# Loading and working the last two rows of each partition as half rows in a row-sum of reciprocals

## The chip, the cores and the metric

The kernel runs on one core of one Trainium2 chip. The metric is the device time of one launch in microseconds (us). Times of single instructions come from one profiled execution of the kernel, counted from the start of its span.

## The reference

```python
# x: [32, 512, 1024] float32, all elements positive
def reference(x):
    return np.sum(1.0 / x, axis=-1).astype(np.float32)      # [32, 512]
```

There are 16,384 rows of 1,024 elements, 67.1 MB in all, and one sum of reciprocals for each.

## The kernel before, in words

**Layout.** Each of the 128 partitions owns 128 consecutive rows. Below, "row c" means row c of every partition at once: a 128x1024 tile of 512 KB. The rows go through `ring`, a buffer of 40 rows. The results collect in `sums` (128x128), and one store at the end (line 260) writes them out.

**Arithmetic.** A row is cut into two halves a and b of 512 elements, and 1/a + 1/b = (a + b) / (ab). So only 512 reciprocals are needed for a row, of the product ab. They are made on ScalarE (ACT) as exp(-ln(S ab)), with S = 2^17. For every row the steps are these, named by the letters that the order list of the last rows uses:

- **P** (GpSimd, POOL, line 212): the product ab. **D** (line 214) is the same on VectorE (DVE). **B** and **V** do it in two steps: TensorE (PE) copies b into PSUM with a matmul by the identity (line 217), and DVE multiplies (line 221).
- **L** (ACT, line 230): ln of the product, in place. **E** (ACT, line 236): exp of its negative.
- **S** (PE, line 226): a + b, as two matmuls by the identity that accumulate in PSUM. Only some rows have it.
- **T** (DVE, helper at line 109): multiply and sum along the row into one column of `sums`. For a row with an S it reads the reciprocal and the PSUM sum, 512 elements. For a row without, it reads the whole row against the reciprocal taken twice, 1,024 elements. In the profile it is one CUSTOM_DVE instruction and one short read of the accumulator.
- **W** and **X** (ACT, lines 248 and 251): for the very last row, ln and exp of all 1,024 elements, with the sum taken by the exp itself.

A "+" behind the number means that one instruction works two neighbouring rows (128x1024 products).

**Stages.** Rows 0 to 103 run in a regular loop (`LOADS`, lines 136 to 182). The last 24 rows, from `LAST = 104`, run by hand: `LAST_LOADS` says in what pieces SyncE (SP) issues the loads (line 188), and `ORDER` gives the instructions in a written order. Each engine takes its own letters out of this list, in list order, and is held to that order. What is at the head of an engine's queue and waits for its input holds up all that stands behind it. Buffers also make waits: the PSUM sums of S have three buffers, the reciprocals that go to PSUM (E of rows without S) have two, and the b copy has one.

Of the kernel before, what the change touches and what calls it, by code (L numbers as in the profile page):

```python
# [11 lines left out]
def kernel(  # L12
# [15 lines left out]
    nc = tc.nc  # L28
    f32 = mybir.dt.float32
    P = 128  # L30
    D = 1024
    H = D // 2
    F = 128

    R = 40
# [10 lines left out]

    LAST = 104
    LAST_LOADS = [2] * 1 + [4] * 1 + [2] * 5 + [1] * 8  # L50
    ORDER = """
        P104 P105 L104+ P107 B106 E104+ V106 P109 B108 L106+ T104 P110+ S108
        E106+ V108 T105 L108+ S109 T106 L110+ P112+ T107 E108+ S112 E110 T108
        L112+ P114+ T109 S113 T110 E111 E112+ T111 L114+ P116 S116 T113 E114+
        T112 P117 L116 T114 P119 B118 L117 E116 S118 V118 E117 P120 T115 L118+
        P121 S119 T116 E118+ T117 P122 L120+ S122 T118 E120+ D123 L122+ T120
        S123 P124 E122+ T119 D125 S125 L124 T122 L125 P126 T121 E124 S126 E125
        T123 L126 T124 W127 E126 T125 X127 T126
    """

    Ln = mybir.ActivationFunctionType.Ln
# [4 lines left out]
    x_v = x.flatten_outer_dims().rearrange("(p f) d -> p f d", p=P)  # L66
# [20 lines left out]
    rpool = ctx.enter_context(  # L87
        tc.tile_pool(name="rpool", bufs=2, space=bass.MemoryType.PSUM)
    )

    ring = opool.tile([P, R, D], f32)
    sums = opool.tile([P, F], f32)
    ident = opool.tile([P, P], f32)
    make_identity(nc, ident)
    keep = tc.keep_in_program_order

    def add(bank, *halves):
        for k, half in enumerate(halves):
            i = nc.tensor.matmul(  # L99
                bank,  # L100
                lhsT=ident,
                rhs=half,
                start=k == 0,
                stop=k == len(halves) - 1,
            )
            keep(i)

    def sum_row(c, row, fac, out=None):
        i = nc.vector.tensor_tensor_reduce(  # L109
            out=row if out is None else out,  # L110
            in0=row,
            in1=fac,
            scale=S,
            scalar=0.0,
            op0=mult,
            op1=plus,
            accum_out=sums[:, c : c + 1],
        )
        keep(i)

    def sum_rows(c, xc, pr, sm, rc):
        m, e = xc.shape[1], len(sm)
        for j in range(e, m):
            row = xc[:, j, :].rearrange("p (h e) -> p h e", h=2)
            sum_row(
                c + j,
                row,
                rc[j - e].unsqueeze(1).to_broadcast([P, 2, H]),
                pr[:, e : e + 2, :] if j == e and e + 1 < m else None,
            )  # L130
        for j in reversed(range(e)):
            sum_row(c + j, pr[:, j, :], sm[j])

    waiting = None
    c0 = 0
    for chunks in LOADS:
        n = sum(m for m, _, _ in chunks)
        xt = ring[:, c0 % R : c0 % R + n, :]
# [3 lines left out]
        for m, e, v in chunks:  # L142
            pr = ppool.tile([P, m, H], f32, tag="ps" if e else "pr")
            for j in range(v):
                b = bpool.tile([P, H], f32, tag="b")
                add(b, xt[:, q + j, H:])
                i = nc.vector.tensor_tensor(  # L147
                    out=pr[:, j, :], in0=xt[:, q + j, :H], in1=b, op=mult
# [6 lines left out]
        for (m, e, v), pr in zip(chunks, made):  # L155
            xc = xt[:, q : q + m, :]
            if v < m:
                i = nc.gpsimd.tensor_tensor(  # L158
                    out=pr[:, v:, :], in0=xc[:, v:, :H], in1=xc[:, v:, H:], op=mult
# [3 lines left out]
            for j in range(e):  # L163
                s = spool.tile([P, H], f32, tag="s")
# [5 lines left out]
            rc = []  # L170
            if e < m:
                r = rpool.tile([P, m - e, H], f32, tag="rc")
# [3 lines left out]
                rc = [r[:, l, :] for l in range(m - e)]  # L176
            if e:
                r = pr[:, :e, :]
# [3 lines left out]
        c0 += n  # L182
    assert c0 == LAST, c0

    c0 = LAST
    for n in LAST_LOADS:
        xt = ring[:, c0 % R : c0 % R + n, :]
        keep(nc.sync.dma_start(out=xt, in_=x_v[:, c0 : c0 + n, :]))
        c0 += n
    assert c0 == F, c0  # L190
    sum_rows(*waiting)

    prs, rs, ss, bs = {}, {}, {}, {}
    order = ORDER.split()
    added = {int(op[1:]) for op in order if op[0] == "S"}
    dead = set()

    def pair(c):
        k = (c - LAST) // 2
        if k not in prs:  # L200
            pr = ppool.tile([P, 2, H], f32, tag=("pr", "ps")[k % 2])
            prs[k] = pr
        return prs[k]

    for op in order:
        kind, c, n = op[0], int(op[1:].rstrip("+")), 1 + op.endswith("+")
        j = (c - LAST) % 2
        rows = ring[:, c % R : c % R + n, :]
        a, b = rows[:, :, :H], rows[:, :, H:]
        pr = None if kind in "WX" else pair(c)[:, j : j + n, :]  # L210
        if kind == "P":
            keep(nc.gpsimd.tensor_tensor(out=pr, in0=a, in1=b, op=mult))  # L212
        elif kind == "D":
            keep(nc.vector.tensor_tensor(out=pr, in0=a, in1=b, op=mult))  # L214
        elif kind == "B":
            bb = bpool.tile([P, H], f32, tag="b")
            add(bb, b[:, 0, :])
            bs[c] = bb
        elif kind == "V":
            keep(  # L220
                nc.vector.tensor_tensor(  # L221
                    out=pr[:, 0, :], in0=a[:, 0, :], in1=bs[c], op=mult
                )
            )
        elif kind == "S":
            s = spool.tile([P, H], f32, tag="s")
            add(s, a[:, 0, :], b[:, 0, :])
            ss[c] = s
        elif kind == "L":
            keep(nc.scalar.activation(out=pr, in_=pr, func=Ln, scale=S))  # L230
        elif kind == "E":
            r = pr
            if c not in added:
                r = rpool.tile([P, n, H], f32, tag="rc")
                rs.update({c + l: r[:, l, :] for l in range(n)})
            keep(nc.scalar.activation(out=r, in_=pr, func=Exp, scale=-1.0))  # L236
            if n == 2:
                dead.add((c - LAST) // 2)
        elif kind == "T" and c in added:
            sum_row(c, pr[:, 0, :], ss[c])  # L240
        elif kind == "T":
            row = rows[:, 0, :].rearrange("p (h e) -> p h e", h=2)
            k = (c - LAST) // 2
            to = prs[k] if k in dead else None
            dead.discard(k)
            sum_row(c, row, rs[c].unsqueeze(1).to_broadcast([P, 2, H]), to)
        elif kind == "W":
            keep(nc.scalar.activation(out=rows, in_=rows, func=Ln))  # L248
        elif kind == "X":
            keep(  # L250
                nc.scalar.activation(
                    out=rows,
                    in_=rows,
                    func=Exp,
                    scale=-1.0,
                    accum_out=sums[:, c : c + 1],
                )
            )
# [32 lines left out]
```

## Time and profile before

| | |
|---|---|
| median of 6 runs | 169.5 us (169.03 to 170.33) |
| the profiled execution | 169.71 us, of which the span of instructions is 167.7 us |
| busy in the span | DVE 135.7 us (81%), ACT 133.8 us (80%), POOL 130.1 us (78%), PE 108.3 us (65%) |
| loads | 67.11 MB, 401 GB/s over the span |
| product on POOL, 1,024 and 512 elements | 2372 and 1280 ns |
| T with 1,024 and 512 elements | 1217 and 682 ns |
| ln on ACT, 1,024 and 512 elements | 1048 and 624 ns |

The page gives busy time for each engine over the whole span and a strip of 40 slices of 4.2 us each. The rows touched by the change are worked in the last 30 us of the span, so the strip and the instructions in order of time at its end say more than the averages. One instruction's duration overlaps a little with its neighbour's on the same engine: two T of 1,024 elements start 1.14 us apart, not 1.22.

### The profile page before, as it was taken

Reading aid. Unit: us, or ns where it says so; the run is one execution under the profiler, and the core shown is the slowest. Engines: PE = TensorE matmul, PEld = TensorE weight load, DVE = VectorE, ACT = ScalarE, POOL = GpSimd, SP = SyncE. Lnnn points to the kernel's source line nnn. Section 1 sums busy time; section 2 is a strip of 40 time slices with the busy share of each in tenths; the row PEclk is TensorE's granted clock in tenths of the full one; section 3 lists DMA queues with packets and bytes.
Section 4 is the critical chain, followed back from the end, with each engine's and each line's share of the span. In section 5 each row is a group of like instructions: output and inputs, shape, how many; then the busy total and the mean of one; then the engine's idle time right before and its main releaser. Section 6 shows DMA issues by size and latency. Waiting matters only on the chain.

```text
span 167.7 us, 1139 instructions
## 1 busy us (share of the span) xinstructions
PE 108.3 (65%) x204; PEld 42.9 (26%) x204; DVE 135.7 (81%) x272; ACT 133.8 (80%) x137; POOL 130.1 (78%) x73
## 2 busy tenths in 40 slices
PE   0007739194774709664395915935999996998990
PEld 0003213031322204221141302402444442433430
DVE  0001697989979798997989897898699999999994
ACT  3001887978789796879979786899899999999994
POOL 1007959699796959969696994999999997999630
PEclk9999987959789975899759996995799999999999
DMA  6999999999999999999999999999999999999910
GB/s 203 422 438 430 414 438 430 446 422 414 446 416 438 391 422 446 430 432 438 438 430 430 422 406 422 430 432 430 424 426 420 424 420 422 420 412 410 409 77 18
DMA packets 4614, 67.23 MB, mean 401 GB/s; under 512 B 512, under 2 KB 640, under 8 KB 1664
## 3 DMA queue, kind: packets, MB, share of 16 engines
q1 hardware_dynamic: 4608, 67.18, 94.9%
q14 instruction: 5, 0.04, 0.1%
q8 instruction: 1, 0.02, 0.0%
HBM read 67.11 MB, written 0.07 MB: 401 GB/s over the span
## 4 chain that ended last, share of the span: by engine, by line
DMA 67%; ACT 11%; POOL 6%; DVE 6%; PE 4%; issue 3%; SPq 1%; ACTq 1%; POOLq 0%
DMA ring<-in_x_dram 67%; POOL pr L158 6%; ACT pr L169 3%; DVE ring L109 3%; ACT pr L230 3%; PE s L99 2%; DVE pr L109 2%; ACT pr L236 2%; SPq L139 1%; ACT r L174 1%; ACT r L236 1%; ACT pr L179 1%; PE b L99 1%; PE bb L99 1%; ACT ring L248 1%
## 5 line engine op out<-in xcount | busy, mean ns | idle before, releaser
L158 POOL TENSOR_TENSOR pr<-ring 128x1024 f32<-128x1024 f32 (+1 forms) x52 | 107.2, 2098 | 27.2 <-DMA ring<-in_x_dram 27.2
L99 PE MATMUL s<-ring,ident 128*128 128x512 f32 x172 | 88.4, 662 | 5.8 <-DVE sums L109 5.7
L169 ACT ACTIVATE pr<-pr 128x1024 f32<-128x1024 f32 x52 | 54.6, 1051 | 28.4 <-POOL pr L158 27.8
L109 DVE CUSTOM_DVE_ANT_1 pr<-ring,r 128x1024 f32<-128x1024 f32 x40 | 48.8, 1221 | 9.4 <-ACT r L174 9.1
L109 DVE CUSTOM_DVE_ANT_1 ring<-ring,r 128x1024 f32<-128x1024 f32 x44 | 53.5, 1217 | 0.0
L99 PEld LDWEIGHTS s<-ring,ident 128*128 128x128 f32 x172 | 36.6, 217 | 58.5 <-issue 41.1
L99 PE MATMUL b<-ring,ident 128*128 128x512 f32 x26 | 19.8, 851 | 47.6 <-DMA ring<-in_x_dram 47.6
L174 ACT ACTIVATE r<-pr 128x1024 f32<-128x1024 f32 x36 | 37.0, 1028 | 1.1
L109 DVE CUSTOM_DVE_ANT_0 pr<-pr,s 128x512 f32<-128x512 f32 x43 | 27.9, 682 | 0.0
L212 POOL TENSOR_TENSOR pr<-ring 128x512 f32<-128x512 f32 (+1 forms) x15 | 22.2, 1499 | 4.2 <-DMA ring<-in_x_dram 3.8
L147 DVE TENSOR_TENSOR pr<-ring,b 128x512 f32<-128x512 f32 x13 | 8.9, 686 | 19.8 <-PE b L99 19.6
L99 PEld LDWEIGHTS b<-ring,ident 128*128 128x128 f32 x26 | 5.4, 247 | 57.0 <-DMA ring<-in_x_dram 36.6
L179 ACT ACTIVATE pr<-pr 128x1024 f32<-128x1024 f32 x16 | 16.9, 1058 | 0.5
L230 ACT ACTIVATE pr<-pr 128x1024 f32<-128x1024 f32 (+1 forms) x14 | 12.4, 897 | 0.5 <-DVE pr L221 0.5
L109 DVE DVE_READ_ACCUMULATOR2_ANT sums<- 128x1 f32 x127 | 10.5, 83 | 0.0
L236 ACT ACTIVATE r<-pr 128x1024 f32<-128x1024 f32 (+1 forms) x8 | 6.4, 804 | 0.1
L236 ACT ACTIVATE pr<-pr 128x1024 f32<-128x1024 f32 (+1 forms) x7 | 6.0, 863 | 0.1
L99 PE MATMUL bb<-ring,ident 128*128 128x512 f32 x6 | 3.4, 644 | 2.0 <-DMA ring<-in_x_dram 1.0
L221 DVE TENSOR_TENSOR pr<-ring,bb 128x512 f32<-128x512 f32 x3 | 2.1, 687 | 0.3 <-PE bb L99 0.2
L99 PEld LDWEIGHTS bb<-ring,ident 128*128 128x128 f32 x6 | 0.9, 188 | 4.5 <-DMA ring<-in_x_dram 2.7
L70 ACT ACT_TABLE_LOAD x1 | 1.3, 1283 | 0.7 <-PEq L275 0.7
L214 DVE TENSOR_TENSOR pr<-ring 128x512 f32<-128x512 f32 x2 | 1.4, 686 | 0.0
(9 smaller groups left out, 3.2 us busy)
## 6 DMA issues: line engine op xcount, KB each, us to landing
ring<-in_x_dram SPq DMA_DIRECT2D x10, 4096.0 KB, 37.2
ring<-in_x_dram SPq DMA_DIRECT2D x7, 2048.0 KB, 35.7
ring<-in_x_dram SPq DMA_DIRECT2D x6, 1024.0 KB, 30.6
ring<-in_x_dram SPq DMA_DIRECT2D x8, 512.0 KB, 14.4
out_dram<-sums SPq DMA_DIRECT2D x1, 64.0 KB, 1.5
```

The source lines that it names most:

```text
L99: i = nc.tensor.matmul(bank, lhsT=ident, rhs=half, start=k == 0, stop=k == len(halves) - 1,)
L109: i = nc.vector.tensor_tensor_reduce(out=row if out is None else out, in0=row, in1=fac, scale=S, scalar=0.0, op0=mult, op1=plus, accum_out ...
L139: keep(nc.sync.dma_start(out=xt, in_=x_v[:, c0 : c0 + n, :]))
L147: i = nc.vector.tensor_tensor(out=pr[:, j, :], in0=xt[:, q + j, :H], in1=b, op=mult)
L158: i = nc.gpsimd.tensor_tensor(out=pr[:, v:, :], in0=xc[:, v:, :H], in1=xc[:, v:, H:], op=mult)
L169: keep(nc.scalar.activation(out=pr, in_=pr, func=Ln, scale=S))
L174: nc.scalar.activation(out=r, in_=pr[:, e:, :], func=Exp, scale=-1.0)
L179: keep(nc.scalar.activation(out=r, in_=r, func=Exp, scale=-1.0))
L212: keep(nc.gpsimd.tensor_tensor(out=pr, in0=a, in1=b, op=mult))
L221: nc.vector.tensor_tensor(out=pr[:, 0, :], in0=a[:, 0, :], in1=bs[c], op=mult)
L230: keep(nc.scalar.activation(out=pr, in_=pr, func=Ln, scale=S))
L236: keep(nc.scalar.activation(out=r, in_=pr, func=Exp, scale=-1.0))
```

## The change

The last two rows, 126 and 127, become four half rows, numbered 126 to 129 (126 and 127 are the halves of row 126, 128 and 129 those of row 127). `place` maps such a number to its row and half.

- **Loads.** A half row is loaded on its own (256 KB, 2 KB in a partition). Rows 118 and 119, which came as one load of two rows, come as two loads. The list has 18 loads instead of 15.
- **Work on a half row.** Its 512 elements are cut into quarters of 256. P, L, E, S and T work on 256 products; a T without S reads 512 elements.
- **Chained sums.** The two halves of a row add into the same column of `sums`: the T of the second half takes the first half's sum as its starting value.
- **The list.** Row 127 has no W and X any more. The other rows change too: which product is made where (P104 and P105 as one instruction, P108 and P109 too, V for 106, 110 and 116, only one D, for 123), which rows have an S (108, 109, 112, 113, 115, 118, 119, 121, 124, 125 and the half rows 127, 128, 129), which ln and exp are paired, and the order.

```diff
-    LAST_LOADS = [2] * 1 + [4] * 1 + [2] * 5 + [1] * 8
+    HALVES = 126
+    LAST_LOADS = [2] * 1 + [4] * 1 + [2] * 4 + [1] * 12
     ORDER = """
-        P104 P105 L104+ P107 B106 E104+ V106 P109 B108 L106+ T104 P110+ S108
-        E106+ V108 T105 L108+ S109 T106 L110+ P112+ T107 E108+ S112 E110 T108
-        L112+ P114+ T109 S113 T110 E111 E112+ T111 L114+ P116 S116 T113 E114+
-        T112 P117 L116 T114 P119 B118 L117 E116 S118 V118 E117 P120 T115 L118+
-        P121 S119 T116 E118+ T117 P122 L120+ S122 T118 E120+ D123 L122+ T120
-        S123 P124 E122+ T119 D125 S125 L124 T122 L125 P126 T121 E124 S126 E125
-        T123 L126 T124 W127 E126 T125 X127 T126
+        P104+ L104+ P107 B106 E104+ V106 P108+ L106+ T104 B110 E106+ T105 S108
+        P111 L108+ V110 T106 L110+ P112+ S109 E108+ T107 E110+ S112 T108 P114
+        T109 L112+ T111 S113 P115 L114 E112+ T110 P117 L115 B116 T112 E114
+        S115 P118 V116 E115 T113 L116+ P119 T114 S118 E116+ T115 P120 L118+
+        T117 S119 P121 L120 T116 E118+ P122 S121 L121 T118 E120 T119 L122 D123
+        E121 T120 L123 P124 S124 E122 T121 E123 P125 T122 L124 S125 E124 P126
+        T123 L125 P127 L126 S127 E125 T124 P128 E126 T125 S128 L127 P129 L128
+        T126 E127 S129 L129 T127 E128 E129 T128 T129
     """
...
-    def sum_row(c, row, fac, out=None):
+    def sum_row(c, row, fac, out=None, more=False):
         i = nc.vector.tensor_tensor_reduce(
...
-            scalar=0.0,
+            scalar=sums[:, c : c + 1] if more else 0.0,
...
+    def load(u, n):
+        c, h = place(u)
+        if u >= HALVES and n == 1:
+            half = slice(h * H, h * H + H)
+            keep(nc.sync.dma_start(out=ring[:, c % R, half], in_=x_v[:, c, half]))
...
+    def place(u):
+        return (u, 0) if u < HALVES else divmod(u + HALVES, 2)
...
+        row, h = place(c)
+        w = H if c < HALVES else H // 2
...
+            rows = ring[:, row % R, :].rearrange("p (u e) -> p u e", u=2)
+            rows = rows[:, h : h + n, :]
+        a, b = rows[:, :, :w], rows[:, :, w:]
...
         elif kind == "T" and c in added:
-            sum_row(c, pr[:, 0, :], ss[c])
+            sum_row(row, pr[:, 0, :], ss[c], None, h)
...
-            sum_row(c, row, rs[c].unsqueeze(1).to_broadcast([P, 2, H]), to)
+            sum_row(row, ab, rs[c].unsqueeze(1).to_broadcast([P, 2, w]), to, h)
```

More of the change, by code (lines that the diff above doesn't have):

```diff
@@ L183 @@
     assert c0 == LAST, c0
-    c0 = LAST
+    def load(u, n):
[3 more added lines that the diff above has]
+            keep(nc.sync.dma_start(out=ring[:, c % R, half], in_=x_v[:, c, half]))
+        else:
+            m = place(u + n)[0] - c
+            xt = ring[:, c % R : c % R + m, :]
+            keep(nc.sync.dma_start(out=xt, in_=x_v[:, c : c + m, :]))
+    def place(u):
+        return (u, 0) if u < HALVES else divmod(u + HALVES, 2)
+    u = LAST
     for n in LAST_LOADS:
[L187 to L190, printed above, removed]
+        load(u, n)
+        u += n
+    assert place(u) == (F, 0), u
     sum_rows(*waiting)
@@ L207 @@
         j = (c - LAST) % 2
-        rows = ring[:, c % R : c % R + n, :]
-        a, b = rows[:, :, :H], rows[:, :, H:]
-        pr = None if kind in "WX" else pair(c)[:, j : j + n, :]
+        row, h = place(c)
+        w = H if c < HALVES else H // 2
+        if c < HALVES:
+            rows = ring[:, row % R : row % R + n, :]
+        else:
+            rows = ring[:, row % R, :].rearrange("p (u e) -> p u e", u=2)
+            rows = rows[:, h : h + n, :]
+        a, b = rows[:, :, :w], rows[:, :, w:]
+        pr = None if kind in "WX" else pair(c)[:, j : j + n, :w]
         if kind == "P":
@@ L216 @@
             bb = bpool.tile([P, H], f32, tag="b")
-            add(bb, b[:, 0, :])
-            bs[c] = bb
+            add(bb[:, :w], b[:, 0, :])
+            bs[c] = bb[:, :w]
         elif kind == "V":
@@ L226 @@
             s = spool.tile([P, H], f32, tag="s")
-            add(s, a[:, 0, :], b[:, 0, :])
-            ss[c] = s
+            add(s[:, :w], a[:, 0, :], b[:, 0, :])
+            ss[c] = s[:, :w]
         elif kind == "L":
@@ L233 @@
             if c not in added:
-                r = rpool.tile([P, n, H], f32, tag="rc")
+                rc = rpool.tile([P, n, H], f32, tag="rc")
+                r = rc[:, :, :w]
                 rs.update({c + l: r[:, l, :] for l in range(n)})
@@ L239 @@
         elif kind == "T" and c in added:
-            sum_row(c, pr[:, 0, :], ss[c])
+            sum_row(row, pr[:, 0, :], ss[c], None, h)
         elif kind == "T":
-            row = rows[:, 0, :].rearrange("p (h e) -> p h e", h=2)
+            ab = rows[:, 0, :].rearrange("p (h e) -> p h e", h=2)
             k = (c - LAST) // 2
-            to = prs[k] if k in dead else None
+            to = prs[k][:, :, :w] if k in dead else None
             dead.discard(k)
-            sum_row(c, row, rs[c].unsqueeze(1).to_broadcast([P, 2, H]), to)
+            sum_row(row, ab, rs[c].unsqueeze(1).to_broadcast([P, 2, w]), to, h)
         elif kind == "W":
```

## The prediction

> **What bounds the kernel now.** I read the strip of 40 slices first, then the end of the instructions in order of time, engine by engine, and then the waits of the loads.
>
> ```profile
> DVE  0001697989979798997989897898699999999994
> ACT  3001887978789796879979786899899999999994
> POOL 1007959699796959969696994999999997999630
> DMA  6999999999999999999999999999999999999910
> ```
>
> A slice is 4.2 us. The loads are at nine tenths or more from the second slice, and stop in slice 38 of 40. DVE and ACT then work on for nearly two more slices. So the span is a full stream of loads, about 160 us, and behind it a backlog of some 4 us. The change can't shorten the stream (the same bytes); it can only alter the end. Who makes the end is in the instructions in order of time (start us, length, engine, line, operation):
>
> ```profile
> 160.84 1.28 POOL L212 TENSOR_TENSOR pr<-ring 128x512 f32<-128x512 f32 x1 [1.22 <-DMA ring<-in_x_dram]
> ...
> 162.76 1.22 DVE L109 CUSTOM_DVE_ANT_1 ring<-ring,r 128x1024 f32<-128x1024 f32 x1
> 163.90 0.08 DVE L109 DVE_READ_ACCUMULATOR2_ANT sums<- 128x1 f32 x1
> 163.90 0.68 DVE L109 CUSTOM_DVE_ANT_0 pr<-pr,s 128x512 f32<-128x512 f32 x1
> 164.51 0.08 DVE L109 DVE_READ_ACCUMULATOR2_ANT sums<- 128x1 f32 x1
> 164.51 0.68 DVE L109 CUSTOM_DVE_ANT_0 pr<-pr,s 128x512 f32<-128x512 f32 x1
> 165.12 0.08 DVE L109 DVE_READ_ACCUMULATOR2_ANT sums<- 128x1 f32 x1
> ```
>
> ```profile
> 164.16 1.04 ACT L251 ACTIVATE ring<-ring 128x1024 f32<-128x1024 f32 x1
> 165.10 0.19 ACT L251 ACTIVATION_READ_ACCUMULATOR ring<-ring 128x1 f32 x1
> ```
>
> POOL starts P126, its last product, as soon as row 126 is there, and is done at 162.1. ACT ends at 165.29 with X127, DVE at 165.20 with T126, both without a break in the last 4 us. The two are a tie, and the store starts at 165.31. From there to the end of the span is 2.4 us, and 2.0 us lie outside the span (169.71 - 167.7); neither changes. So I have to find the time of the last sum after the change, against 165.29.
>
> A second list with full queues can be no better than its work. DVE from T104 (starts at 141.32) to the end: 12 T of 1,024 elements at 1.14 us, 11 T of 512 at 0.61, V108, V118, D123, D125 at 0.605 (all start to start) are 22.8 us, and the breaks in order of time are 0.16 (142.5), 0.16 (151.4), 0.32 (152.7) and 0.35 (157.7), 1.0 in all. 141.3 + 22.8 + 1.0 = 165.1.
>
> ```profile
> SPq L188 <- DMA ring<-in_x_dram: 46.3, 14, 4.5
> ```
>
> This is from the waits of SP: a load of the last rows is issued when the load eight before it has landed. With smaller loads, eight of them hold fewer bytes.
>
> **What the Trainium skill says.** "ScalarE: Activation LUTs", section "What ACT_TABLE_LOAD costs": an ACTIVATE with immediate scale and bias takes 186 ns + 0.833 ns an element, and neighbours overlap by 93 ns. That gives 613 and 1039 ns for 512 and 1,024; the trace has 624 and 1048 for ln. So I take 0.40 us for 256, 0.31 start to start. "VectorE: DVE Perf Modes", section "The DRAIN you can't avoid": a [P,1] result of one DVE instruction that the next takes as scalar operand is read stale unless it waits; the chained sums are that case, so a wait must come. No instruction of the kernel before shows it. "DMA: Bandwidth & Descriptors", section "Why small descriptors are slow": a fixed cost for each packet. The packet records of the trace agree: 161 ns for 4,096 bytes, 313 for 8,192, 613 for 16,384, so some 10 ns are fixed.
>
> **The change, part by part.**
>
> *Loads.* Rows 118 and 119 apart: 16 packets of 161 ns on an engine instead of 8 of 313, +0.07 us. Four half rows: 32 packets of 2,048 bytes, by the line 86 ns, for 16 of 161, +0.18 us. The semaphore of row 127 completed at 161.9 before, so the last half lands near 162.2 (rows come 1.28 us apart, halves 0.69). Three more issues on SP at 0.33 us are nothing. The eight loads in flight behind the last issue (near 154.4) still hold 5.5 rows, 7 us of stream: it does not run dry.
>
> *POOL.* P with 512 elements is 1.28 us, with 1,024 2.37, so 256 is 0.74 by the line (0.69 start to start). Row 124 lands at about 158.2 and P124 starts at 158.35. Then nothing waits for a load: P124, P125 at 1.24 each, P126 to P129 at 0.69 each, end at 163.7. POOL ended at 162.1 before, so its end moves by 1.6 us, since P125 was a D on DVE and row 127 had no product. The last half is there at 162.2 and P129 starts at 162.9: the +0.25 us of the loads costs nothing as long as it stays under 0.6 us.
>
> *ACT.* W127 and X127 go (2.27 us with the accumulator's read), and eight operations of 256 come for them and for L126, E126. From the walk (each operation starts when its engine is free and its input is there, 0.03 to 0.1 us after it): L126 161.67, E125 161.97, E126 162.48, L127, L128, E127, then L129 at 163.74, held up by P129 for 0.1 us, E128, E129 to 164.73. ACT leaves the end: 0.56 us earlier.
>
> *DVE.* D125 goes to POOL; row 127, which cost DVE nothing while X summed it, brings two T. V110 and V116 stand for V108 and V118. Now: 12 T of 1,024 (104 to 107, 110, 111, 114, 116, 117, 120, 122, 123) 13.70 us; 10 of 512 with an S 6.09; T126 with 512 elements 0.61; T127 to T129 with 256, by the line through 1217 and 682 ns 0.415 long, 0.34 start to start, 1.02; V110, V116, D123 1.82. Sum 23.2 us, **0.4 more than before**, from T104 at 141.2 (after E104, whose place in the queue of ACT is unchanged). Breaks in the walk: V116 0.13 (B116's matmuls), T118 0.30 (E118, behind L120, which waits for P120 at 154.5), others 0.05, and at the end T127 0.15, T128 0.12 (E128), T129 0.15. The two at T127 and T129 are the chain: each starts only after the accumulator read before it, 0.07 us behind its end, where neighbours otherwise overlap by 0.07. Behind T127 stand T128 and T129, behind T129 the store. 141.2 + 23.2 + 0.9 = 165.3, and with the last read 165.4.
>
> *PE.* S127 to S129 on 256 columns are 0.86 us each by half of a full S (1.72). S129 ends at 164.7 and T129 needs it only at 165.0.
>
> The same walk on the old list ends at 165.1 on DVE and 165.3 on ACT, within 0.1 us of the trace.
>
> **Costs that no row shows.** A chained T reads a pointer operand and waits for its own engine: at the least nothing over the 0.15 above (an ACT exp behind its own ln starts 0.03 after it), at the most 0.5 us each, about the length of a separate instruction. I take +0.1 each; the first 0.1 falls partly into T128's wait for E128, so the end is 165.5. A quarter product on POOL: 0.64 (half of 1.28) to 0.90 (were 0.35 fixed); the walk then ends at 165.3 to 166.1. ACT at 256: 0.1 more each gives 165.7. Loads of half rows 1 us late give 165.8.
>
> 165.5 - 165.29 = +0.2 us: 169.9 for an execution like the profiled one, and **169.7 us** against the median of 169.5, which is 0.2 below the profiled 169.71. What ACT gains is given away because DVE, tied with it, gets more work and two waits.
>
> **The rivals.**
>
> *Slower: the chained sums.* T126 to T129 end the queue of DVE one behind the other, with nothing between T128 and T129, so every price of a chained sum is the kernel's. For it: the trace shows no DVE instruction that waits for the one just ahead. Against it: ACT does this (ln, then exp of the same tile) at 0.03 us. At 0.6 us over my walk for each, the end is 166.5 and the time 170.7. From about 0.4 each the kernel is over 0.5% slower (0.85 us, about what a measurement of this kernel can tell from no change).
>
> *Faster: the new list closes the breaks.* If T118, V116 and T128 don't wait and the chain costs nothing, 141.2 + 23.2 = 164.4 and 164.6 with the read: 169.0 as a median. For it: the breaks were 1.0 us before, and each hangs on tenths of the walk. Against it: L120 can't pass P120, which follows from rows landing 1.28 us apart. Even this is a gain of only 0.5 us; over 0.85 T104 would have to start earlier, and nothing ahead of it changes.
>
> *POOL as the bound.* P124 to P129 are one chain from the landing of row 124. If quarters cost 0.9 us, POOL ends at 164.3, then L129, E129, T129 one after the other: 166.05, 170.3 as a median. For it: POOL moves 1.6 us towards the end. Against it: its two sizes lie on a line with a fixed part of only 0.19 us.
>
> **How the numbers follow.** Forecast 0.60, chained sums 0.18, POOL 0.10, breaks closed 0.12. Within 0.5% (168.65 to 170.35) are the forecast, most of POOL and of the closed breaks. Slower: the chained sums and the upper part of POOL's, 0.22. Faster: 0.06, a start of T104 that moved together with closed breaks. Same: 0.72. The range reaches from the closed breaks, 169.0, to POOL's bound with some of the chain's, 170.6.
>
> **What would show it.** Right: the last instruction ahead of the store is on DVE, near 165.5; ACT ends about 0.7 us before it; POOL runs six products without a break from about 158.3 to 163.7; T127 and T129 start after the accumulator read before them; durations near 0.74 (POOL), 0.40 (ACT) and 0.42 (T) at 256. Wrong: a chained T that starts 0.3 us or more behind the read, POOL quarters of 0.9 us, a last landing past 162.8, or DVE breaks outside those named.

## The result, and the profile after

The changed kernel is slower: 171.12 us as the median of 34 runs (169.73 to 173.63), against 169.74 for 71 runs of the kernel before (169.03 to 171.03). The ratio is 1.0063, 95% interval 1.0045 to 1.0080. The ratio leaves out the runs over 1.5% above the fastest of the same kernel as disturbed; here those eight runs show the effect itself, so the ratio is on the small side. The record also has the span of instructions of each run, and by the span the 34 runs are two groups: 21 from 167.9 to 169.2 us, the early group, and 13 from 169.9 to 171.4, the late group. (The times alone don't separate so well, because what lies outside the span is mostly 1.9 us but reaches 3.0.) The median time of the early 21 is 170.6 us. The profiled execution took 172.15 us with a span of 170.3 us and belongs to the late group.

The strip of the changed kernel, 40 slices of 4.26 us each:

```profile
DVE  0001797979988897989979897896999998889993
ACT  3002879969787997978789795899999997969891
POOL 1008969597995969699796959999999969998850
DMA  6999999999999999999999999999999999999600
```

The last load lands at 161.92 us, at 161.94 before. What is new is in slices 34 to 38, where DVE and ACT were full before: there are holes in the backlog. The end of DVE, in order of time:

```profile
165.22 0.68 DVE L112 CUSTOM_DVE_ANT_1 ring<-ring,rc 128x512 f32<-128x512 f32 x1
165.83 0.08 DVE L112 DVE_READ_ACCUMULATOR2_ANT sums<- 128x1 f32 x1
166.09 0.48 DVE L112 CUSTOM_DVE_ANT_0 pr<-pr,s,sums 128x256 f32<-128x256 f32 x1 [0.17 <-ACT pr L253]
166.49 0.08 DVE L112 DVE_READ_ACCUMULATOR2_ANT sums<- 128x1 f32 x1
166.49 0.42 DVE L112 CUSTOM_DVE_ANT_0 pr<-pr,s 128x256 f32<-128x256 f32 x1
166.84 0.08 DVE L112 DVE_READ_ACCUMULATOR2_ANT sums<- 128x1 f32 x1
167.09 0.48 DVE L112 CUSTOM_DVE_ANT_0 pr<-pr,s,sums 128x256 f32<-128x256 f32 x1 [0.17 <-DVE sums L112]
167.50 0.08 DVE L112 DVE_READ_ACCUMULATOR2_ANT sums<- 128x1 f32 x1
```

These are T126, T127, T128, T129. DVE is last, as forecast, but at 167.58 instead of 165.5. The two chained sums (with `sums` as an operand) are 0.48 us long against 0.42 for T128, and each starts 0.17 us behind the read ahead of it. ACT and POOL, the columns as above:

```profile
165.88 0.71 ACT L260 ACTIVATE pr<-pr 128x256 f32<-128x256 f32 x2
158.23 5.74 POOL L235 TENSOR_TENSOR pr<-ring 128x512 f32<-128x512 f32 x6 [1.29 <-ACT pr L253]
```

ACT ends at 166.6. POOL runs its six products without a break to 163.96. The late part lies elsewhere: in the waits from 126 us on (who, for whom, us in total, times, longest).

```profile
ACT pr L253 <- POOL pr L235: 1.5, 1, 1.5
DVE pr L244 <- PE bb L102: 1.6, 3, 0.7
```

The second line is the three V, which wait for their copy from PE, 0.7 us the longest. The first is L116+, and it carries the wrong name: L116+ needs P117, which POOL had ended at 150.5, and V116, which DVE ended at 153.00. It starts at 153.09, 0.09 us behind V116, the same distance as for V106 and V110. So both engines stand still for V116, and V116 for PE:

```profile
152.31 0.69 DVE L244 TENSOR_TENSOR pr<-ring,bb 128x512 f32<-128x512 f32 x1 [0.70 <-PE bb L102]
```

V116 starts at 152.31. The sums of the prediction put it near 150.6: T104 at 141.2, 9.3 us of work on DVE from there, and a break of 0.13. PE had been late since B110 (start, length of the group, shape, count, wait):

```profile
139.21 1.12 PE L102 MATMUL bb<-ring,ident 128*128 128x512 f32 x2 [1.21 <-DMA ring<-in_x_dram]
141.79 2.04 PE L102 MATMUL bb<-ring,ident 128*128 128x512 f32 x2 [1.46 <-DMA ring<-in_x_dram]
143.63 3.92 PE L102 MATMUL s<-ring,ident 128*128 128x512 f32 x7
```

The kernel before has B106 and B108 at these places:

```profile
139.40 1.12 PE L99 MATMUL bb<-ring,ident 128*128 128x512 f32 x2 [0.60 <-DMA ring<-in_x_dram]
141.46 1.13 PE L99 MATMUL bb<-ring,ident 128*128 128x512 f32 x2 [0.93 <-DVE pr L221]
```

In the changed kernel B106 takes 1.12 us, and B110, which is the same work, takes 2.04. The record of the granted clock, the share of its full clock that PE gets, says why: one half from 141.72 to 145.13. From there PE is busy without a pause up to 163, so it never makes the loss good.

### The profile page after: what moved, and what is told of

It reads as the page before. It is cut to its first block, busy times and chain, and to the rows that moved or that the text cites. A ratio compares the mean times of both kernels' runs of the same rounds, so it can differ in the third digit from the quotient of the medians.

```text
span 170.3 us, 1184 instructions
## 1 busy us (share of the span) xinstructions
PE 109.5 (64%) x212; PEld 44.9 (26%) x212; DVE 137.1 (80%) x277; ACT 133.5 (78%) x143; POOL 133.2 (78%) x77
## 4 chain that ended last, share of the span: by engine, by line
DMA 70%; ACT 11%; DVE 9%; POOL 4%; issue 2%; PE 1%; DVEq 0%; SPq 0%; ACTq 0%; POOLq 0%
DMA ring<-in_x_dram 70%; ACT pr L253 4%; DVE pr L112 4%; DVE ring L112 4%; POOL pr L161 3%; ACT rc L260 2%; ACT pr L260 2%; POOL pr L235 1%; ACT pr L172 1%; ACT r L177 1%; PE bb L102 1%; DVE pr L237 1%; DVE pr L244 0%; DVE sums L112 0%; DVEq L112 0%
## 5 line engine op out<-in xcount | busy, mean ns | idle before, releaser
L102 PE MATMUL s<-ring,ident 128*128 128x512 f32 (+1 forms) x180 | 89.3, 646 | 7.7 <-DVE sums L112 7.3
L102 PEld LDWEIGHTS s<-ring,ident 128*128 128x128 f32 x180 | 38.5, 218 | 60.6 <-issue 42.3
L112 DVE CUSTOM_DVE_ANT_1 pr<-ring,r 128x1024 f32<-128x1024 f32 x36 | 44.0, 1221 | 9.8 <-ACT r L177 9.8
L112 DVE CUSTOM_DVE_ANT_1 ring<-ring,r 128x1024 f32<-128x1024 f32 x36 | 43.8, 1217 | 0.0
L112 DVE CUSTOM_DVE_ANT_0 pr<-pr,s 128x512 f32<-128x512 f32 (+1 forms) x43 | 27.7, 676 | 0.6 <-PE s L102 0.6
L235 POOL TENSOR_TENSOR pr<-ring 128x512 f32<-128x512 f32 (+2 forms) x19 | 25.4, 1363 | 3.1 <-DMA ring<-in_x_dram 1.5
L253 ACT ACTIVATE pr<-pr 128x512 f32<-128x512 f32 (+2 forms) x19 | 13.5, 730 | 2.9 <-POOL pr L235 1.5
L112 DVE CUSTOM_DVE_ANT_1 ring<-ring,rc 128x1024 f32<-128x1024 f32 (+1 forms) x9 | 10.3, 1155 | 0.0
L260 ACT ACTIVATE rc<-pr 128x1024 f32<-128x1024 f32 (+2 forms) x9 | 6.8, 755 | 0.2
L260 ACT ACTIVATE pr<-pr 128x512 f32<-128x512 f32 (+2 forms) x10 | 6.7, 680 | 0.0
L112 DVE CUSTOM_DVE_ANT_1 pr<-ring,rc 128x1024 f32<-128x1024 f32 x4 | 4.9, 1216 | 0.0
```

The source lines that it names most:

```text
L102: i = nc.tensor.matmul(bank, lhsT=ident, rhs=half, start=k == 0, stop=k == len(halves) - 1,)
L112: i = nc.vector.tensor_tensor_reduce(out=row if out is None else out, in0=row, in1=fac, scale=S, scalar=sums[:, c : c + 1] if more else 0. ...
```

## The experiments

Two theories stood against each other. **G, the clock gate**: B110 at the head of PE's queue waits for rows 110 and 111, PE is idle too long, its clock is halved for 3.4 us, and PE delivers late. **C, chained sums and quarters**: the small operations cost more than the lines through the larger ones give. L (half-row loads late), W (the order of the last waits) and K (two products holding each other up) came up on the way. The medians of the kernel before beside these runs were 169.2 to 169.3 us.

**after_again**: the changed kernel, for a second profile.

> The changed kernel once more, for a second profile. Theory G (clock gate): in the list of the change B110 stands alone at the head of PE's queue until rows 110 and 111 land, PE is idle from 140.3 to 141.8, the granted clock falls to one half for a window of 3.4 us and PE, in order and without slack, delivers V116's copy 1.6 us late. Where the window falls differs from run to run, so the time is spread over 2 us or more: 169.8 to 172.5, median 171.1. If this profile has full clock from 140 to 146, its last sum is near 165.8 and its time near 170.1 to 170.3. Rival C (chained sums and quarters): every run has the same extra, the spread is that of the kernel before, about 1.5 us, and a profile with full clock there still ends near 167.5.

Measured: six runs from 169.81 to 170.46 us, three from 172.03 to 172.55, ratio 1.0082 (1.0050 to 1.0114). The profile (172.13 us) again has half clock, from 141.93 to 145.34. By the span, too, they are two groups with nothing between them, 168.0 to 168.6 and 169.9 to 170.0. That fits G, not C.

**after_fill**: filler work for PE.

```diff
-        P104+ L104+ P107 B106 E104+ V106 P108+ ...
+        P104+ L104+ P107 K104 B106 K105 E104+ V106 P108+ ...
...
+        if kind == "K":                       # a copy that nobody reads
+            s = spool.tile([P, H], f32, tag="s")
+            add(s, a[:, 0, :])
```

> The changed kernel with two filler copies on PE (0.86 us each at full clock), one ahead of B106 and one between B106 and B110, where PE sat idle; nobody reads them. Theory G: the granted clock stays at 1.0 from 138 to 146, B110's matmuls take 0.6 to 0.7 us instead of 1.1 to 1.2, V116 starts by 151.0 instead of 152.3, D123 is 0.69 us again, median 170.0 to 170.4, spread below that of the changed kernel. Rival C: no change, 171.1. Rival L (half-row loads late): no change either.

Measured: 169.94 us (169.84 to 170.64, 6 runs), ratio 1.0047 (1.0034 to 1.0060). Full clock, V116 at 150.40, D123 0.689 us, last read ended at 165.30. The median is just under the expected band. By the span (167.9 to 168.8) none of the six runs is late. Six runs are few, since only four in ten of the changed kernel are late; the two kernels with these fillers at the end of this section add 30 runs, none of them late either. So more work on PE makes the late group go. There remain 0.6 us against the kernel before.

**after_b108**: one part of the list undone.

```diff
-        ... V106 P108+ L106+ T104 B110 E106+ T105 S108
-        P111 L108+ V110 T106 L110+ ...
+        ... V106 P109 B108 L106+ T104 P110+ S108 E106+
+        V108 T105 L108+ T106 L110+ ...
```

> The changed kernel with one part of its list undone: row 108's product by B108 and V108 (its row has landed by 139.4), P109 alone and P110+ as a pair, as in the kernel before, instead of P108+, B110, V110 and P111. Theory G: PE does not wait for rows 110 and 111 with an empty queue, idle time ahead of 142 falls from 2.7 to about 1.5 us, clock 1.0, median 170.0 to 170.4. Rival C and rival L: 171.1.

Measured: 169.91 us (169.65 to 170.93, 7 runs), ratio 1.0045 (1.0028 to 1.0061); full clock, and no run late by its span (168.0 to 169.0). It was 0.1 us under the expected band, otherwise as G says.

**before_b110**: the same part put into the kernel before.

```diff
-        ... V106 P109 B108 L106+ T104 P110+ S108
-        E106+ V108 T105 L108+ S109 T106 L110+ ...
+        ... V106 P108+ L106+ T104 B110 S108 E106+
+        T105 P111 L108+ V110 S109 T106 L110+ ...
```

> The kernel before with only that part of the change: P108+, B110, P111, V110 instead of P109, B108, V108, P110+; no half rows, no chained sums. Theory G: PE is idle for 1.4 us ahead of B110, clock of one half after it in many runs, S and V118 late, median 170.3 to 171.3 and a wider spread than before. Rivals C and L: 169.7, as before.

Measured: 15 runs from 168.99 to 169.59 us and five from 171.27 to 171.48; median 169.42, ratio 1.0029 (1.0004 to 1.0053). The median is a miss, the second group is a hit: B110 alone, without a half row in the kernel, brings runs 2 us late, here in one of four (spans of 167.2 to 167.5 and 169.3 to 169.4). The profile fell on the first group, so that the clock halves in this kernel's late runs is likely but wasn't seen.

**after_look3 and after_look4**: the changed kernel profiled twice more, to see both groups in one kernel.

> The changed kernel, one more look. Theory G: either the clock of PE is one half for 3.4 us from about 142, V116 starts after 152, D123 takes 1 us, and the time is 171.6 or more; or it is full from 138 to 160, V116 starts by 151, D123 takes 0.69 us, the last read ends near 165.4 and the time is 169.8 to 170.5. Rival (another cause of the spread): a late run with full clock, or an early one with half clock.

> The changed kernel, one more look, with the same expectation as after_look3: half clock from about 142 and 171.6 us or more, or full clock and 169.8 to 170.5 us; the rival is a run that pairs them the other way round.

Measured: after_look3 took 169.89 us, after_look4 171.84. Each fell into one group. Busy time by stretch (us, then busy and count of PE, PE's weight loads, DVE, ACT, POOL, then the clock of PE, the loads' share, GB/s), first after_look3, then after_look4:

```profile
142.00:145.50 3.50, 3.50 (x10) 1.53 (x9) 3.50 (x6) 3.50 (x4) 3.41 (x3) 1.00 1.01 421
```

```profile
142.00:145.50 3.50, 3.50 (x6) 1.32 (x5) 2.97 (x6) 3.09 (x4) 3.38 (x3) 0.59 1.00 417
```

PE is busy all the time in both, but gets 10 matmuls done in one and 6 in the other. B110, after the same wait, and V116 of after_look3:

```profile
141.55 1.10 PE L102 MATMUL bb<-ring,ident 128*128 128x512 f32 x2 [1.46 <-DMA ring<-in_x_dram]
```

```profile
150.41 0.69 DVE L244 TENSOR_TENSOR pr<-ring,bb 128x512 f32<-128x512 f32 x1 [0.20 <-PE bb L102]
```

V116 is 1.9 us earlier than in the profile of the result. The last read ends at 165.32 in after_look3 and at 167.28 in after_look4. All four profiles of the changed kernel pair half clock with a late end or full clock with an early one: same kernel, same queue, and 2 us between them. Together with the fillers, which keep the clock full and make the late group go, this shows theory G for the 2 us. It doesn't cover what the early group loses.

**What a window of PE needs.** The record of the granted clock changes in steps of 3.41 us. Windows of this length, laid over all sixteen traces from 18 to 160 us, give PE's busy share in each from the matmul records. Of the windows at full clock, those up to 0.41 busy (the last is 0.409, b108_spare5 from 90.3 us) were all followed by half clock, those over 0.47 by full clock. Between, both occur: full clock after 0.413 (the kernel before, from 88.5), half clock after 0.422 (before_halfloads, from 137.7), 0.438 (b108_spare5, from 138.1) and 0.466 (after_again, from 138.5). Some matmul records can be missing, so the shares may be a little low. For the window ahead of B110: 0.33 in the profile of the result, 0.47 in after_again, 0.33 in after_look4, and 0.56 in after_look3. PE's two pauses, 1.1 to 1.2 us ahead of B106 and 1.45 ahead of B110, lie 2.4 us apart in the middle. In the profile of the result the window from 138.3 to 141.7 holds most of both; in after_look3 the window from 138.9 to 142.4 holds the second alone. In the old list row 108 of B108 was there with row 106, and the second pause is 0.8 to 0.9 us in the traces of the kernel before, before_d125late and before_spare3, the first 0.6 to 1.1. All three keep full clock here.

**D123.** In the late group V116 makes DVE late, and D123, which stood in POOL's pause between P122 and P124, falls beside P124 and P125. First DVE, then POOL (P124 and P125 as one group), in the profile of the result:

```profile
159.01 1.04 DVE L237 TENSOR_TENSOR pr<-ring 128x512 f32<-128x512 f32 x1
```

```profile
158.23 2.97 POOL L235 TENSOR_TENSOR pr<-ring 128x512 f32<-128x512 f32 x2 [1.29 <-ACT pr L253]
```

and the same two products of POOL in after_look3, where D123 had ended before them and took 0.69:

```profile
157.99 2.52 POOL L235 TENSOR_TENSOR pr<-ring 128x512 f32<-128x512 f32 x2 [1.29 <-ACT pr L260]
```

**before_d125late** tried this without the clock: in the kernel before, D125 beside P126.

```diff
-        ... D125 S125 L124 T122 L125 P126 T121 ...
+        ... S125 L124 T122 D125 L125 P126 T121 ...
```

> The kernel before with one operation moved: D125, a product on DVE of two operands in SBUF, behind T122 instead of ahead of it, so that it falls beside P126 on POOL instead of into POOL's pause. Theory K (these two hold each other up): D125 takes 0.9 to 1.1 us instead of 0.69 and P126 1.6 to 1.8 instead of 1.28, without any change of the clock of PE; the end comes 0.3 to 0.8 us later. Rival (they were long in the changed kernel because of the late queue or the clock): both as before.

Measured, in one run: 170.31 us against 169.33, clock full, last read ended at 165.85. DVE and POOL:

```profile
160.44 0.69 DVE L214 TENSOR_TENSOR pr<-ring 128x512 f32<-128x512 f32 x1
```

```profile
160.50 1.76 POOL L212 TENSOR_TENSOR pr<-ring 128x512 f32<-128x512 f32 x1 [1.22 <-DMA ring<-in_x_dram]
```

POOL's product took 0.48 us longer, as expected; DVE's was not touched, which was not expected. In this pair DVE had started first, by 0.06 us. In the late group, where P124 was already running, D123 took longer too. So it looks as if the one that starts first keeps its speed. The other traces with such a pair bear this out (us from the start of each span):

| trace | end of POOL's first product | DVE's product | end of POOL's next product |
|---|---|---|---|
| the result | 159.50 | 159.01 to 160.05 | 161.19 |
| after_again | 159.18 | 158.72 to 159.73 | 160.88 |
| after_look4 | 159.20 | 158.72 to 159.75 | 160.89 |
| b108_spare5 (below) | 159.58 | 158.44 to 160.13 | 161.28 |
| before_d125late | none | 160.44 to 161.12 | 162.27 |

However early DVE's product started, it ended 0.55 us behind the end of POOL's first one, which kept its 1.27 to 1.28 us. And POOL's next product ended 1.14 to 1.15 us behind the end of DVE's. Each seems to get on only when the other has ended, which costs DVE up to 1.0 us. V116, which takes one operand from PSUM, ran its 0.69 us beside POOL's P119 without loss to either (0.69 and 1.27 us, the profile of the result).

**before_spare3**: a part of the remaining 0.6 us. In the traces the time from the store's start to the span's end is 2.37 us for the kernel before and 2.67 for the changed one. Eight semaphores go round the loads; SP waits for them at the end, two at a time, in a fixed order. The kernel before has 31 loads and its store gets the last of the order (110); 34 loads give it the second (105), and more waits are carried out after the store has landed: three in the changed kernel, four in before_spare3.

```diff
+        if c0 == 32:                          # the fifth load; SP then waits for the ring
+            for t in range(3):
+                keep(nc.sync.dma_start(out=spare[:, 8 * t : 8 * t + 8], in_=x_v[:, 0, :8]))
```

> The kernel before with three spare loads of 32 bytes a partition, issued behind the fifth load, when SP waits for the ring anyway; nobody reads them. Eight semaphores go round the loads, so the store of the sums gets semaphore 105, as in the changed kernel with its 34 loads, instead of 110. Theory W (order of the last waits): SP ends the program by waiting for its semaphores in a fixed order; 110 stands last there and 105 second, so four waits come after the store's landing instead of none. From the store's start to the end of the span 2.7 us instead of 2.4, all before the store as it was: slower by 0.3 us than the kernel before. Rival (the longer end belongs to the changed kernel's work, or the longer time to its sums): no difference.

Measured: 169.69 us (169.46 to 170.43, 21 runs) against 169.32, ratio 1.0021 (1.0011 to 1.0031). From the store to the end 2.64 us, and the last read at 164.87. Theory W holds: three idle loads lengthen the end of the kernel before by 0.3 us (0.37 in the medians) without touching its work.

**before_halfloads**: the loads of the change alone, `LAST_LOADS = [2] * 1 + [4] * 1 + [2] * 4 + [1] * 8 + [0.5] * 4` in the kernel before, where 0.5 is a half row.

> The kernel before with the loads of the change alone: rows 118 and 119 apart, rows 126 and 127 as two half rows each; all work as before, on whole rows. 34 loads, so the store of the sums stands on semaphore 105. Theory G+W: the loads themselves cost nothing that shows (the last landing 0.2 to 0.3 us later, before ACT needs row 127), the end after the store is 0.3 us longer: 0.3 to 0.5 us slower than before, in a narrow spread. Rival L (small loads late): 0.8 us or more slower.

Measured: 169.71 us (169.58 to 170.07, 9 runs), ratio 1.0026 (1.0016 to 1.0036); store to end 2.74 us, the last half row landed at 161.64. The loads cost little more than the 0.3 us of their number, so L falls. By chance its profile (170.03 us, 0.3 over the median of its runs) has half clock from 141.13, behind a pause of 1.41 us ahead of B106. V118 starts at 153.11 in it, 0.55 us later than in before_spare3. So half clock can come in the old list too, and costs less there: PE still stands idle for 0.44 us ahead of B118 in the profile of the kernel before, and for 0.45 in before_spare3, which takes up a part of the loss. What takes up the rest was not traced.

**b108_spare5, b108_swap, b108_swap_spare5**: repairs on after_b108. The swap separates the chained sums:

```diff
-        T126 E127 S129 L129 T127 E128 E129 T128 T129
+        E128 T126 E127 S129 L129 T128 E129 T127 T129
```

> The changed kernel with row 108's product by B108 and V108 again (the kernel of the run after_b108), and five spare loads behind the fifth load, so that the store gets semaphore 110 as in the kernel before. Theory W: 2.4 us from the store to the end, 0.3 us faster than after_b108, so 0.2 to 0.4 us slower than before. Rival: as after_b108, 0.6 us slower than before.

> The kernel of after_b108 with the last sums in another order, T126 T128 T127 T129 and E128 ahead of E127, so that each chained sum has another T between it and the sum it goes on from. Theory C (a chained sum waits 0.17 us behind the accumulator read ahead of it and runs 0.06 us longer): the two waits go, 0.25 us each against a T that follows directly; the last read comes 0.4 to 0.5 us earlier, the kernel is 0.1 to 0.3 us slower than before. Without theory C: as after_b108, 0.6 us slower than before.

> All three together: B108, the last sums in the order T126 T128 T127 T129, and the store on semaphore 110. If the clock gate, the chain and the order of the last waits are the whole of the loss, it is within 0.2 us of the kernel before, perhaps 0.2 us faster; if something else in the half rows costs time, it stays 0.3 us or more slower.

Measured: b108_swap 169.75 us (169.43 to 172.17, 18 runs), ratio 1.0025 (1.0012 to 1.0037). T127 now starts with T128's read instead of 0.17 behind one; T128 waits for E128, and T129 0.05 us behind its read. From the read of T126 to the end of the last, 1.57 us instead of 1.74: a gain of 0.17, less than half of what was expected, and the kernel is 0.4 us slower than before, not 0.1 to 0.3. One of its 18 runs is late by its span (170.2): taking B110 out makes late runs rare, but not impossible. The two kernels with five spare loads were a miss: 170.47 us (169.56 to 172.90, 16 runs), ratio 1.0056 (1.0036 to 1.0077), and 170.15 (169.49 to 173.15, 22 runs), ratio 1.0051 (1.0032 to 1.0070). Their tail is 2.40 us as W says. But late runs are back, five of 16 and four of 22 by the span. The profile of b108_spare5 has half clock from 141.52, behind a pause of 1.44 us ahead of B106, with a last read at 168.70 and D123 at 1.70 us. The 128 pieces of 32 bytes of each spare load may have held up the stream: row 106 landed at 139.21 in both profiles, at 138.80 to 139.00 in the other runs of this section that have its time. The first two profiles, of the kernel before and of the result, had it at 139.36 and 139.17 without any spare load, so this isn't shown.

**b108_fill_swap and b108_fill_swap_sem**: all repairs, the second with spare loads of one partition only.

> The kernel of b108_swap with the two filler copies on PE, one ahead of B106 and one between B106 and B108, where its PE still sat idle for 0.7 and 0.8 us. Theory G: the runs over 171 us go, 169.4 to 170.0 us, 0.2 to 0.4 us slower than before. Rival: the spread stays.

> b108_fill_swap with five spare loads of 32 bytes in one partition, so that the store stands on semaphore 110 and the stream of loads is hardly held up (in the runs with spare loads of 128 partitions it was, by 0.3 us). Theory W: 2.4 us from the store to the end, 0.3 us faster than b108_fill_swap, so within 0.2 us of the kernel before, on either side. If it is 0.3 us slower or more, something in the half rows costs that none of the three repairs touches.

Measured: 169.81 us (169.53 to 171.01, 9 runs), ratio 1.0038 (1.0020 to 1.0056), and 169.49 us (169.26 to 171.19, 21 runs), ratio 1.0022 (1.0005 to 1.0039). In both profiles PE has no pause over 0.1 us between 120 and 156 us, and by the span no run is late (up to 168.8 and 168.5). The tail of the second is 2.53 us, not 2.4. Of its 21 runs 13 lie between 169.26 and 169.53, near the kernel before (169.33), and the other eight go up to 171.19. No profile fell on one of those, but their spans are only 167.4 to 168.5: taken together, two thirds of what they lose lies outside the span (2.0 to 3.0 us against the usual 1.8), where no trace sees it. No version beat the kernel before.

## Why the prediction was wrong

- **PE was priced at one speed.** The step that failed is the one on PE and on the break at V116: "V116 0.13 (B116's matmuls)", and a full S at 1.72 us whatever stood ahead of it. The prediction doesn't name B110 and its wait for rows 110 and 111; it asked how long PE's work is, not what a wait does to the engine. "TensorE: Matmul & The Clock Gate", section "Part 1: The HAM clock gate (the "warmup" mystery)", says that the array's clock is halved after an idle window and that the window, 3,413 ns, runs freely. The trace agrees on the 3.41 us and on the one half; but 53 to 67% of idle time in a window was enough here. The page was not in the prediction, and the profile that it had showed no half clock from 120 us to the end of the work. In the three late profiles V116 starts 1.6 to 1.9 us later than in after_look3, with D123's 0.32 to 0.35 on top, and the last read ends 1.9 to 2.3 us later.
- **"Neither changes"** for what lies after the store: in the span it grew by 0.30 us. The three loads more were counted by their issue time and not by what their number does to the last waits. The 2.0 us outside the span didn't stay either: 1.87 us is the median of the changed kernel's runs against 2.0 for the kernel before beside the experiments; no run shows why.
- **Chained sums**: taken at 0.15 of break in the walk and 0.1 on top. Measured 0.174 behind the read and 0.06 longer, against 0.07 in the walk: 0.17 on top. The mechanism was right, the size 0.07 each too small, 0.14 in all. As the rival for "slower" it would have needed 0.4 each.
- **The rest of the walk came near.** In after_look3, with full clock, POOL's six products took 5.28 us from 157.99 (158.35 to 163.7 forecast), a quarter product 0.74 us, ACT's 256 elements 0.40, T128 0.42, and the last half row landed at 161.64 (162.2 forecast). The last read ended at 165.32, which looks like the 165.5 forecast, but that is partly luck: T104 started at 140.74 in it, not at 141.2. In before_spare3, which does the old list's work, T104 started at 140.73 and the last read ended at 164.87. So the new list ends 0.45 us later with full clock, where +0.2 was forecast; the 0.14 of the chained sums is a part of the difference.
- **POOL as the bound** and the **closed breaks**: neither came.

So +0.2 fails even with full clock. There the loss is 0.6 us (after_fill) to 0.7 (after_look3): 0.45 in the sums and 0.3 after the store, less 0.13 outside the span. In the early groups of the result and of after_again it is 0.9 by the medians, and the 0.2 to 0.3 more is open. The late group adds 2 us in 13 of the 34 runs. The median, +1.4, is made of both and is no run's own price.

## What to carry to other kernels

When a queue is reordered, look at how long each engine now stands idle, not only at what it delivers late: an engine whose clock follows its load can lose more after the pause than in it, and by chance from run to run. Runs that fall into two groups call for profiles of both before any mean is explained, and the spans can separate groups that the times blur. And count what a new load or buffer does to fixed sequences such as the waits at the program's end.

## What the runs showed of the hardware that I had not expected

- In fixed windows of 3.41 us, PE's clock was halved after each window that was up to 41% busy and after some up to 47% (sixteen traces, 18 to 160 us); a pause of 1.45 us can be enough beside one of 1.2. With two filler copies of 0.86 us the clock stayed full in the three kernels that had them.
- A product of two SBUF operands on DVE and one on POOL side by side: the one that started first kept its time (DVE 0.69 us, POOL 1.28), the other ended a fixed time behind it (DVE 0.55 us, POOL 1.14 to 1.15), so that DVE took 1.01 to 1.70 us and POOL 1.73 to 1.76.
- The semaphore of the last store is worth 0.27 us in the kernel before: from the store to the end 2.37 us where it is the last that SP waits for, 2.64 where it is the second. Over all traces the two are 2.37 to 2.53 and 2.64 to 2.78.
